# Paired value products issued as one group in alternating column halves, and a compress stage for keys and values side by side

## The chip, the cores and the metric

The kernel runs on one core of one Trainium2 chip. The metric is device time in microseconds (us), the median over runs. One execution was also recorded by the profiler; its trace gives for every engine when each instruction started and how long it took.

## The reference, cut to what matters

A two-layer decoder trunk over 256 positions with model width 1024, all in f32. Layer 0 mixes three attention groups that read one normalised input: sparse attention (8 query heads, 2 key/value groups, with a compressed branch, a selected branch and a window branch), block attention (8 heads) and attention into 256 memory rows (4 heads). Layer 1 has retention (4 heads) and memory attention again. With 256 positions the selected, window and block masks all come down to causal attention. What the change touches is this:

```python
def nsa_compress(a, pe, w1, w2):          # once for keys, once for values
    blocks = a[:, idx] + pe[...]          # 15 windows of 32 positions, stride 16
    hid = silu(einsum('bnlgd,lde->bnge', blocks, w1))
    return einsum('bnge,ef->bngf', hid, w2)

# per head, in each attention branch
p = masked_softmax(q @ k.T * scale)
o = p @ v                                 # the value product
# sparse attention: o = g0 * o_compressed + g1 * o_selected + g2 * o_window
```

## The kernel before, in words

Activations and weights of the projections are each split into two f32r parts (`split`, L102: a cast on ScalarE at L106, a subtraction on VectorE at L107), and every product is three matmuls (`mm3`, L117, lines L119 to L121). Attention probabilities and values stay f32; the trace shows every plain f32 matmul as two records, each with a weight load of its own.

Heads go in pairs. `causal_pair` (L398) does one pair of one branch: per head and per half of the queries a masked maximum on VectorE (L405), an exponential on ScalarE (L407), a scaling, then three transposes on TensorE into the only `t` bank (L178) and a copy of the bank to `pt` on ScalarE (L419). Then come four value products: for key tile 0 both heads (L421, 256 columns each), for key tile 1 both heads (L423, 128 columns each). Head 0 of the pair has 64 weight columns and writes PSUM partitions 0 to 63, head 1 writes 64 to 127, both in the bank `o`, of which there is one. `mem_attention` (L439) does the same for the memory group without a mask, with four value products of 256 columns (L469). `sparse_pair` (L577) opens its bank with the compressed branch: for each head one product from 15 rows of `vcR` and `pcT` into that head's 64 partitions (L585), and then adds two `causal_pair`s. There are four sparse pairs (two `causal_pair`s each), four block pairs (one each) and two memory pairs in each layer: 16 groups of four value products in all.

`compress` (L494) projects 280 columns, transposes, and then runs a loop over keys (i = 0) and values (i = 1): four additions on VectorE build the windows (L526), 16 accumulated matmuls with 64 weight columns and 30 moving columns (L530), then exponential, add, reciprocal and product for SiLU on 64 partitions (L533 to L537, L543), then the second weight (L538 for keys, L547 for values) and copies to `kcBD` (L540) and `vcR` (L549).

The instructions are not executed in the order of the text. The tile framework, opened with `schedule_with_timeline_sim=True` (L967), plans each engine's order at build time by simulated durations: what is ready by its simulation goes ahead, and projections fill the stretches in which attention waits. On the chip each engine then takes its instructions in that fixed order. All weights come in through SyncE's DMA queue (`load`, L86).

Of the kernel before, what the change touches and what calls it, by code (L numbers as in the profile page):

```python
# [12 lines left out]
AF = mybir.ActivationFunctionType  # L13
# [3 lines left out]
P = 128  # L17
# [34 lines left out]
def trunk(  # L52
# [33 lines left out]
    def load(t, src):  # L86
        nc.sync.dma_start(t, src)
        return t


    def rsqrt(y, v, n):
# [83 lines left out]
    def transposes(blocks, tag="t"):  # L175
        b = bank(tag)
        for i, a in enumerate(blocks):
            PE.transpose(b[:, i * P : (i + 1) * P], a, ident)  # L178
        return b[:, : P * len(blocks)]
# [218 lines left out]
    def causal_pair(ss, v, gate, o, first, last):  # L398

        p = tl("p", [P, 2, 512], 2)  # L400
        mx = tl("mx", [P, 2, 2], 3)
        sm = tl("sm", [P, 2, 2], 3)
        for hh in range(2):
            for tok, a in enumerate(SPAN):
                V.tensor_tensor_reduce(p[:, hh, a], ss[hh][tok], cpak[:, C_CAUSAL + a.start : C_CAUSAL + a.stop], -1.0,  # L405
                                       3e38, ALU.add, ALU.min, mx[:, hh, tok : tok + 1])
                S.activation(p[:, hh, a], p[:, hh, a], AF.Exp, bias=mx[:, hh, tok : tok + 1], scale=-1.0,  # L407
                             accum_out=sm[:, hh, tok : tok + 1])
        pt = tl("pt", [P, 2, 512], 2)
        for hh in range(2):  # L410
            V.reciprocal(sm[:, hh], sm[:, hh])
            if gate is not None:
                V.tensor_tensor(sm[:, hh], sm[:, hh], gate[:, :, hh], ALU.mult)
            for tok, a in enumerate(SPAN):
                if 2 * hh + tok == (0 if gate is None else 3):
                    S.activation(p[:, hh, a], p[:, hh, a], AF.Copy, scale=sm[:, hh, tok : tok + 1])
                else:
                    V.tensor_scalar(p[:, hh, a], p[:, hh, a], sm[:, hh, tok : tok + 1], None, op0=ALU.mult)
            S.copy(pt[:, hh, :384], transposes([p[:, hh, i * P : (i + 1) * P] for i in range(3)]))  # L419
        for hh in range(2):  # L420
            PE.matmul(o[hh * 64 : hh * 64 + 64, 0:T], v(hh, 0), pt[:, hh, 0:T], start=first, stop=False)  # L421
        for hh in range(2):
            PE.matmul(o[hh * 64 : hh * 64 + 64, P:T], v(hh, 1), pt[:, hh, T : T + P], start=False, stop=last)  # L423

    def gated(o, szT, y, kt):

# [12 lines left out]
    def mem_attention(eqT, kT, kl, v, szT, y):  # L439
        for pr in range(2):  # L440
# [15 lines left out]
            for hh in range(2):  # L456
                V.reciprocal(sm[:, hh], sm[:, hh])
                for tok in range(2):
                    a = slice(tok * T, (tok + 1) * T)
                    if 2 * hh + tok == 3:  # L460
                        S.activation(p[:, hh, a], p[:, hh, a], AF.Copy, scale=sm[:, hh, tok : tok + 1])
                    else:
                        V.tensor_scalar(p[:, hh, a], p[:, hh, a], sm[:, hh, tok : tok + 1], None, op0=ALU.mult)
                S.copy(pt[:, hh], transposes([p[:, hh, tok * T + kt * P : tok * T + (kt + 1) * P]
                                              for kt in range(2) for tok in range(2)]))
            for kt in range(2):
                for hh in range(2):
                    c = (2 * pr + hh) * 64
                    PE.matmul(o[hh * 64 : hh * 64 + 64, :T], v[:, kt, c : c + 64], pt[:, hh, kt * T : (kt + 1) * T],  # L469
                              start=kt == 0, stop=kt == 1)  # L470
            gated(o, szT[:, pr], y, pr)

    kS = kL = vsw = qT = nq = gates = kcBD = vcR = pcT = yn = eqS = szm = mh = ml = rstdm = rbm = memkS = memkL = memv = ym = szb = mq = mk = mkL = mvt = yb = kS1 = kL1 = v1m = None
# [20 lines left out]
    def compress():  # L494
        nonlocal gates, kcBD, vcR
        ps = project(w280, 0, (xh, xl), 280)
        w1t = [load(tl("v4", [P, 16, 64], NV), w1[i]) for i in range(2)]
        w2t = load(tl("yf", [P, T], 2)[:64, :P], w2)
        gates = tl("gates", [P, 2, 24])
        b = bank("o")  # L500
        for tok in range(2):
# [10 lines left out]

        kcBD = tl("kcbd", [P, 30])
        G.memset(kcBD, 0.0)
        srep = tl("yf", [P, T], 2)[:64].rearrange("p (g a n) -> p g a n", g=2, a=4)
        G.memset(srep, 0.0)
        vcR = tl("vcr", [P, 2, 64])
        for i in range(2):
            blk = tl("tmp2", [P, 512], 3)[:, :480].rearrange("p (a g n) -> p a g n", a=16, g=2)
            pe = vect[:, (V_PEK, V_PEV)[i] : (V_PEK, V_PEV)[i] + 32].rearrange("p (b l) -> p b l", b=2)  # L520
            for l2 in range(2):
                for g in range(2):
                    gs = slice(g * 64, (g + 1) * 64)
                    win = b[gs, i * T + l2 : i * T + T]
                    src = bass.AP(tensor=win.tensor, offset=win.offset, ap=[list(win.ap[0]), [2, 16], [16, 15]])
                    V.tensor_tensor(blk[l2 * 64 : (l2 + 1) * 64, :, g, :], src,  # L526
                                    pe[gs, l2].unsqueeze(2).to_broadcast([64, 16, 15]), ALU.add)
            hb = bank("s")
            for lp in range(16):
                PE.matmul(hb[:64, :30], w1t[i][:, lp], blk[:, lp].rearrange("p g n -> p (g n)"),  # L530
                          start=lp == 0, stop=lp == 15)
            h = tl("hid", [64, 30], 2)
            S.activation(h, hb[:64, :30], AF.Exp, scale=-1.0)  # L533
            V.tensor_scalar(h, h, 1.0, None, op0=ALU.add)
            V.reciprocal(h, h)
            if i == 0:
                V.tensor_tensor(h, hb[:64, :30], h, ALU.mult)  # L537
                PE.matmul(hb[:64, 64:94], w2t[:, 0:64], h, start=True, stop=True)  # L538
                for g in range(2):
                    S.copy(kcBD[g * 64 : (g + 1) * 64, g * 15 : (g + 1) * 15], hb[:64, 64 + g * 15 : 79 + g * 15])  # L540
            else:
                for g in range(2):
                    V.tensor_tensor(srep[:, g, :, :15],  # L543
                                    hb[:64, g * 15 : (g + 1) * 15].unsqueeze(1).to_broadcast([64, 4, 15]),
                                    h[:, g * 15 : (g + 1) * 15].unsqueeze(1).to_broadcast([64, 4, 15]), ALU.mult)
                for g in range(2):
                    PE.matmul(hb[:, 128 + g * 64 : 192 + g * 64], srep[:, g].rearrange("p a b -> p (a b)"),  # L547
                              w2t[:, 64:128], start=True, stop=True)
                S.copy(vcR.rearrange("p g f -> p (g f)"), hb[:, 128:256])  # L549

    def compressed_scores():
        nonlocal qT, gates, kcBD, pcT
# [24 lines left out]
    def sparse_pair(pr):  # L577
# [1 line left out]
        if pr == 0:  # L579
            yn = tl("y", [P, 2, 4, T], 2, F32R)  # L580
        o = bank("o")
        for g in range(2):
            n = 2 * pr + g
            cr = slice(32 * (n % 4), 32 * (n % 4) + 15)
            PE.matmul(o[g * 64 : g * 64 + 64, :T], vcR[cr, g], pcT[cr, n // 4], start=True, stop=False)  # L585
        ss = branch_scores(nq[pr // 2][:, pr % 2], kS, kL)
        for br in (1, 2):
            causal_pair(ss[br - 1],
# [382 lines left out]
```

## Time and profile before

| | |
|---|---|
| time, median of 3 runs (lowest to highest) | 450.48 us (450.01 to 451.08) |
| the profiled execution: its own time | 450.25 us |
| its span, first to last instruction | 448.5 us |
| around the span | 1.75 us |
| TensorE busy, records | 435.9 us (97%), 2586 |
| weight loads busy | 367.8 us (82%) |
| VectorE busy | 331.7 us (74%) |
| ScalarE busy | 257.3 us (57%) |
| GpSimd busy | 9.4 us (2%) |
| mean granted TensorE clock | 0.997 |

Busy time of TensorE counts the whole of each record, and records overlap, since the next matmul starts while the one before is still draining. So 97% doesn't say that the array streams all that time: what a matmul costs is read from the distance between the starts of two that follow each other.

### The profile page before, as it was taken

How to read it: one execution, taken by the hardware profiler on the slowest of the kernel's cores; microseconds unless marked ns; L12 is line 12 of the kernel's file. 1: busy time of each engine (PE TensorE's matmuls, PEld its weight loads, DVE VectorE, ACT ScalarE, POOL GpSimd, SP SyncE). 2: the span in 40 equal slices, each digit the busy share in tenths (PEclk: the TensorE clock that was granted, in tenths of full speed). 3: DMA queues.
4: the chain of work that ended last, by engine and by line, in shares of the span. 5: the costliest groups of instructions: out<-in, count | busy, mean ns of one | idle time of the engine just before them, and what ended most of it. 6: DMA issues, size and time to landing. Idle time of an engine off the chain costs nothing.

```text
span 448.5 us, 7101 instructions
## 1 busy us (share of the span) xinstructions
PE 435.9 (97%) x2586; PEld 367.8 (82%) x2586; DVE 331.7 (74%) x762; ACT 257.3 (57%) x472; POOL 9.4 (2%) x22
## 2 busy tenths in 40 slices
PE   8999999999999799999999999999999999999994
PEld 6988899888777467667999888888998888888883
DVE  4898989997888766756898776577877478764725
ACT  5756557947656966854646625464543356453714
POOL 0000100001101000000010000000000000000000
PEclk9999999999999999999999999999999999999998
DMA  8965765853343134222546334455545545555402
GB/s 281 391 227 185 214 235 176 274 187 134 102 142 132 56 117 165 95 94 95 176 145 214 142 117 166 164 178 160 190 145 186 187 142 203 159 209 198 142 0 94
DMA packets 22146, 74.20 MB, mean 165 GB/s; under 512 B 2720, under 2 KB 3424, under 8 KB 22112
## 3 DMA queue, kind: packets, MB, share of 16 engines
q1 hardware_dynamic: 21536, 72.92, 47.1%
q10 hardware_dynamic: 576, 0.84, 0.6%
q8 instruction: 20, 0.33, 0.3%
q14 instruction: 14, 0.11, 0.1%
HBM read 72.70 MB, written 1.05 MB: 164 GB/s over the span
## 4 chain that ended last, share of the span: by engine, by line
PE 91%; DVE 3%; ACT 3%; DMA 1%; issue 1%; ACTq 0%
PE pj L119 23%; PE pj L120 23%; PE pj L121 22%; PE t L178 3%; PE o L421 2%; PE s L372 1%; PE s L120 1%; PE s L119 1%; PE o L469 1%; PE s L121 1%; PE tr L120 1%; PE tr L119 1%; PE s L373 1%; PE tr L121 1%; DMA vec<-in_vec 1%
## 5 line engine op out<-in xcount | busy, mean ns | idle before, releaser
L107 DVE TENSOR_TENSOR wlo<-raw,whi 128x1024 fp32r<-128x1024 f32 (+2 forms) x124 | 145.1, 1174 | 58.2 <-ACT whi L106 57.2
L106 ACT CAST whi<-raw 128x1024 fp32r<-128x1024 f32 (+2 forms) x124 | 124.6, 1007 | 94.0 <-PE pj L121 28.0
L120 PE MATMUL pj<-wlo,big 128*128 128x512 f32 (+2 forms) x264 | 99.0, 375 | 0.1
L121 PE MATMUL pj<-whi,big 128*128 128x512 f32 (+2 forms) x264 | 98.3, 373 | 0.0
L119 PE MATMUL pj<-whi,big 128*128 128x512 f32 (+2 forms) x264 | 92.7, 376 | 0.0
L119 PE MATMUL pj<-big,whi 128*128 128x256 f32 x288 | 80.6, 285 | 0.7 <-ACT big L198 0.6
L120 PE MATMUL pj<-big,whi 128*128 128x256 f32 x288 | 81.1, 285 | 0.0
L121 PE MATMUL pj<-big,wlo 128*128 128x256 f32 x288 | 80.0, 285 | 0.5 <-DVE wlo L107 0.4
L120 PEld LDWEIGHTS pj<-wlo,big 128*128 128x128 f32 x264 | 49.7, 188 | 9.1 <-issue 0.8
L119 PEld LDWEIGHTS pj<-big,whi 128*128 128x128 f32 x288 | 54.7, 191 | 2.5 <-ACT big L198 1.0
L121 PEld LDWEIGHTS pj<-whi,big 128*128 128x128 f32 x264 | 49.7, 188 | 8.4
L119 PEld LDWEIGHTS pj<-whi,big 128*128 128x128 f32 x264 | 49.2, 188 | 8.4 <-issue 0.4
L120 PEld LDWEIGHTS pj<-big,whi 128*128 128x128 f32 x288 | 55.0, 191 | 0.8 <-issue 0.4
L121 PEld LDWEIGHTS pj<-big,wlo 128*128 128x128 f32 x288 | 54.3, 191 | 1.0 <-DVE wlo L107 0.9
L407 ACT ACTIVATE p<-p,mx 128x256 f32<-128x256 f32 (+1 forms) x48 | 21.4, 448 | 1.5 <-DVE mx L405 1.3
L178 PE MATMUL t<-cst,p 128*128 128x128 f32 x104 | 18.0, 281 | 1.0 <-ACT pt L419 0.6
L405 DVE CUSTOM_DVE_ANT_0 p<-s,cst 128x256 f32<-128x256 f32 (+1 forms) x48 | 14.6, 353 | 4.9 <-PE t L178 4.4
L419 ACT COPY pt<-t 128x384 f32<-128x384 f32 x24 | 11.5, 479 | 10.7 <-PE t L178 10.6
L178 PEld LDWEIGHTS t<-cst,p 128*128 128x128 f32 x104 | 11.8, 140 | 6.0 <-issue 3.3
L372 PE MATMUL s<-v,v 128*128 128x256 f32 (+2 forms) x48 | 14.7, 326 | 0.2 <-DVE mx L405 0.2
L120 PE MATMUL pj<-wlo,y 128*128 128x512 f32 x36 | 14.2, 396 | 0.0
L373 PE MATMUL s<-v,v 128*128 128x256 f32 (+2 forms) x48 | 13.4, 298 | 0.0
(292 smaller groups left out, 649.5 us busy)
## 6 DMA issues: line engine op xcount, KB each, us to landing
raw<-in_w SPq DMA_DIRECT2D x91, 512.0 KB, 3.8
raw<-in_wout SPq DMA_DIRECT2D x28, 512.0 KB, 3.6
v<-in_xtok SPq DMA_DIRECT2D x4, 512.0 KB, 6.2
raw<-in_w SPq DMA_DIRECT2D x4, 280.0 KB, 3.4
v<-in_w SPq DMA_DIRECT2D x2, 512.0 KB, 7.0
raw<-in_memT SPq DMA_DIRECT2D x2, 512.0 KB, 3.5
raw<-in_memtok SPq DMA_DIRECT2D x2, 512.0 KB, 4.6
v<-in_grow SPq DMA_DIRECT2D x2, 512.0 KB, 5.5
```

Of the source, the lines that this page charges most:

```text
L106: S.copy(hi, raw)
L107: V.tensor_tensor(lo, raw, hi.bitcast(F32), ALU.subtract)
L119: PE.matmul(ps, lh, rh, start=start, stop=False, skip_group_check=shared)
L120: PE.matmul(ps, lh, rl, start=False, stop=False, skip_group_check=shared)
L121: PE.matmul(ps, ll, rh, start=False, stop=stop, skip_group_check=shared)
L178: PE.transpose(b[:, i * P : (i + 1) * P], a, ident)
L372: PE.matmul(s, q, k, start=True, stop=False)
L373: PE.matmul(s, q, kl, start=False, stop=True)
L405: V.tensor_tensor_reduce(p[:, hh, a], ss[hh][tok], cpak[:, C_CAUSAL + a.start : C_CAUSAL + a.stop], -1.0, 3e38, ALU.add, ALU.min, mx[:, hh ...
L407: S.activation(p[:, hh, a], p[:, hh, a], AF.Exp, bias=mx[:, hh, tok : tok + 1], scale=-1.0, accum_out=sm[:, hh, tok : tok + 1])
L419: S.copy(pt[:, hh, :384], transposes([p[:, hh, i * P : (i + 1) * P] for i in range(3)]))
L421: PE.matmul(o[hh * 64 : hh * 64 + 64, 0:T], v(hh, 0), pt[:, hh, 0:T], start=first, stop=False)
```

## The change

The four value products of a pair become one list that is handed to a new helper, `side_by_side`. It issues them in the same order as the lines before (key tile 0 of head 0, of head 1, key tile 1 of head 0, of head 1), but ties the first to the second head's `pt` copy by an explicit dependency, and each later one behind the one before it on TensorE. The compressed branch of a sparse pair becomes one matmul with 128 weight columns: `vcR` is now 128 x 2 x 128 with zeros outside the blocks, so that the product of head g uses its own 15 rows alone. In `compress` the two loops of 16 matmuls are interleaved, keys into partitions 0 to 63 and values into 64 to 127 of one bank; SiLU runs once on 128 partitions; `w2` is loaded twice, once for each half of the partitions; `vcR` is cleared on GpSimd and filled by four copies.

```diff
@@ -86,6 +86,21 @@
     def load(t, src):
         nc.sync.dma_start(t, src)
         return t
+
+    def after(ins, *others):
+
+        for other in others:
+            tc.add_manual_dep(ins.ins, other.ins.name,
+                              mybir.DependencyInfo(mybir.DependencyClass.Sync, mybir.DependencyReason.DATA), reason="pair")
+
+    def side_by_side(todo, *others):
+
+        for i, (out, lhs, rhs, start, stop) in enumerate(todo):
+            ins = PE.matmul(out, lhs, rhs, start=start, stop=stop)
+            if i == 0:
+                after(ins, *others)
+            else:
+                tc.keep_in_program_order(ins)
 
 
     def rsqrt(y, v, n):
@@ -416,11 +431,9 @@
                     S.activation(p[:, hh, a], p[:, hh, a], AF.Copy, scale=sm[:, hh, tok : tok + 1])
                 else:
                     V.tensor_scalar(p[:, hh, a], p[:, hh, a], sm[:, hh, tok : tok + 1], None, op0=ALU.mult)
-            S.copy(pt[:, hh, :384], transposes([p[:, hh, i * P : (i + 1) * P] for i in range(3)]))
-        for hh in range(2):
-            PE.matmul(o[hh * 64 : hh * 64 + 64, 0:T], v(hh, 0), pt[:, hh, 0:T], start=first, stop=False)
-        for hh in range(2):
-            PE.matmul(o[hh * 64 : hh * 64 + 64, P:T], v(hh, 1), pt[:, hh, T : T + P], start=False, stop=last)
+            got = S.copy(pt[:, hh, :384], transposes([p[:, hh, i * P : (i + 1) * P] for i in range(3)]))
+        side_by_side([(o[hh * 64 : hh * 64 + 64, kt * P : T], v(hh, kt), pt[:, hh, kt * T : kt * P + T],
+                       first and kt == 0, last and kt == 1) for kt in range(2) for hh in range(2)], got)
 
     def gated(o, szT, y, kt):
 
@@ -461,13 +474,10 @@
                         S.activation(p[:, hh, a], p[:, hh, a], AF.Copy, scale=sm[:, hh, tok : tok + 1])
                     else:
                         V.tensor_scalar(p[:, hh, a], p[:, hh, a], sm[:, hh, tok : tok + 1], None, op0=ALU.mult)
-                S.copy(pt[:, hh], transposes([p[:, hh, tok * T + kt * P : tok * T + (kt + 1) * P]
-                                              for kt in range(2) for tok in range(2)]))
-            for kt in range(2):
-                for hh in range(2):
-                    c = (2 * pr + hh) * 64
-                    PE.matmul(o[hh * 64 : hh * 64 + 64, :T], v[:, kt, c : c + 64], pt[:, hh, kt * T : (kt + 1) * T],
-                              start=kt == 0, stop=kt == 1)
+                got = S.copy(pt[:, hh], transposes([p[:, hh, tok * T + kt * P : tok * T + (kt + 1) * P]
+                                                    for kt in range(2) for tok in range(2)]))
+            side_by_side([(o[hh * 64 : hh * 64 + 64, :T], v[:, kt, (2 * pr + hh) * 64 : (2 * pr + hh + 1) * 64],
+                           pt[:, hh, kt * T : (kt + 1) * T], kt == 0, kt == 1) for kt in range(2) for hh in range(2)], got)
             gated(o, szT[:, pr], y, pr)
 
     kS = kL = vsw = qT = nq = gates = kcBD = vcR = pcT = yn = eqS = szm = mh = ml = rstdm = rbm = memkS = memkL = memv = ym = szb = mq = mk = mkL = mvt = yb = kS1 = kL1 = v1m = None
@@ -495,7 +505,9 @@
         nonlocal gates, kcBD, vcR
         ps = project(w280, 0, (xh, xl), 280)
         w1t = [load(tl("v4", [P, 16, 64], NV), w1[i]) for i in range(2)]
-        w2t = load(tl("yf", [P, T], 2)[:64, :P], w2)
+        w2t = tl("yf", [P, T], 2)[:, :P]
+        for i in range(2):
+            load(w2t[64 * i : 64 * i + 64], w2)
         gates = tl("gates", [P, 2, 24])
         b = bank("o")
         for tok in range(2):
@@ -512,9 +524,11 @@
 
         kcBD = tl("kcbd", [P, 30])
         G.memset(kcBD, 0.0)
-        srep = tl("yf", [P, T], 2)[:64].rearrange("p (g a n) -> p g a n", g=2, a=4)
+        srep = tl("yf", [P, T], 2)[64:].rearrange("p (g a n) -> p g a n", g=2, a=4)
         G.memset(srep, 0.0)
-        vcR = tl("vcr", [P, 2, 64])
+        vcR = tl("vcr", [P, 2, 2, 64])
+        G.memset(vcR, 0.0)
+        blks = []
         for i in range(2):
             blk = tl("tmp2", [P, 512], 3)[:, :480].rearrange("p (a g n) -> p a g n", a=16, g=2)
             pe = vect[:, (V_PEK, V_PEV)[i] : (V_PEK, V_PEV)[i] + 32].rearrange("p (b l) -> p b l", b=2)
@@ -523,30 +537,29 @@
                     gs = slice(g * 64, (g + 1) * 64)
                     win = b[gs, i * T + l2 : i * T + T]
                     src = bass.AP(tensor=win.tensor, offset=win.offset, ap=[list(win.ap[0]), [2, 16], [16, 15]])
-                    V.tensor_tensor(blk[l2 * 64 : (l2 + 1) * 64, :, g, :], src,
-                                    pe[gs, l2].unsqueeze(2).to_broadcast([64, 16, 15]), ALU.add)
-            hb = bank("s")
-            for lp in range(16):
-                PE.matmul(hb[:64, :30], w1t[i][:, lp], blk[:, lp].rearrange("p g n -> p (g n)"),
-                          start=lp == 0, stop=lp == 15)
-            h = tl("hid", [64, 30], 2)
-            S.activation(h, hb[:64, :30], AF.Exp, scale=-1.0)
-            V.tensor_scalar(h, h, 1.0, None, op0=ALU.add)
-            V.reciprocal(h, h)
-            if i == 0:
-                V.tensor_tensor(h, hb[:64, :30], h, ALU.mult)
-                PE.matmul(hb[:64, 64:94], w2t[:, 0:64], h, start=True, stop=True)
-                for g in range(2):
-                    S.copy(kcBD[g * 64 : (g + 1) * 64, g * 15 : (g + 1) * 15], hb[:64, 64 + g * 15 : 79 + g * 15])
-            else:
-                for g in range(2):
-                    V.tensor_tensor(srep[:, g, :, :15],
-                                    hb[:64, g * 15 : (g + 1) * 15].unsqueeze(1).to_broadcast([64, 4, 15]),
-                                    h[:, g * 15 : (g + 1) * 15].unsqueeze(1).to_broadcast([64, 4, 15]), ALU.mult)
-                for g in range(2):
-                    PE.matmul(hb[:, 128 + g * 64 : 192 + g * 64], srep[:, g].rearrange("p a b -> p (a b)"),
-                              w2t[:, 64:128], start=True, stop=True)
-                S.copy(vcR.rearrange("p g f -> p (g f)"), hb[:, 128:256])
+                    got = V.tensor_tensor(blk[l2 * 64 : (l2 + 1) * 64, :, g, :], src,
+                                          pe[gs, l2].unsqueeze(2).to_broadcast([64, 16, 15]), ALU.add)
+            blks.append(blk)
+
+        hb = bank("s")
+        side_by_side([(hb[64 * i : 64 * i + 64, :30], w1t[i][:, lp], blks[i][:, lp].rearrange("p g n -> p (g n)"),
+                       lp == 0, lp == 15) for lp in range(16) for i in range(2)], got)
+        h = tl("hid", [P, 30])
+        S.activation(h, hb[:, :30], AF.Exp, scale=-1.0)
+        V.tensor_scalar(h, h, 1.0, None, op0=ALU.add)
+        V.reciprocal(h, h)
+        V.tensor_tensor(h, hb[:, :30], h, ALU.mult)
+        for g in range(2):
+            V.tensor_copy(srep[:, g, :, :15], h[64:, g * 15 : (g + 1) * 15].unsqueeze(1).to_broadcast([64, 4, 15]))
+        PE.matmul(hb[:64, 64:94], w2t[:64, 0:64], h[:64], start=True, stop=True)
+        for g in range(2):
+            PE.matmul(hb[:, 128 + g * 64 : 192 + g * 64], srep[:, g].rearrange("p a b -> p (a b)"),
+                      w2t[64:, 64:128], start=True, stop=True)
+        for g in range(2):
+            S.copy(kcBD[g * 64 : (g + 1) * 64, g * 15 : (g + 1) * 15], hb[:64, 64 + g * 15 : 79 + g * 15])
+        for a in range(4):
+            rows = slice(32 * a, 32 * a + 15)
+            S.copy(vcR[rows, a // 2, a % 2], hb[rows, 128 + 64 * (a % 2) : 192 + 64 * (a % 2)])
 
     def compressed_scores():
         nonlocal qT, gates, kcBD, pcT
@@ -579,10 +592,7 @@
         if pr == 0:
             yn = tl("y", [P, 2, 4, T], 2, F32R)
         o = bank("o")
-        for g in range(2):
-            n = 2 * pr + g
-            cr = slice(32 * (n % 4), 32 * (n % 4) + 15)
-            PE.matmul(o[g * 64 : g * 64 + 64, :T], vcR[cr, g], pcT[cr, n // 4], start=True, stop=False)
+        PE.matmul(o[:, :T], vcR[:, pr % 2].rearrange("p g f -> p (g f)"), pcT[:, pr // 2], start=True, stop=False)
         ss = branch_scores(nq[pr // 2][:, pr % 2], kS, kL)
         for br in (1, 2):
             causal_pair(ss[br - 1],
```

## Rows read from the trace of the kernel before

**Rows 1.** The page: busy tenths in 40 slices of the span, 11.2 us each.

```profile
PE   8999999999999799999999999999999999999994
DVE  4898989997888766756898776577877478764725
```

**Rows 2.** TensorE's waits: for whom, us in total, times, longest.

```profile
PE o L469 <- ACT pt L464: 1.4, 1, 1.4
PE o L421 <- ACT pt L419: 0.8, 2, 0.6
```

**Rows 3.** Windows by stage: busy PE, PEld, DVE, ACT, POOL; clock, DMA.

```profile
58.00:95.00 37.00, 37.00 (x293) 34.33 (x292) 35.34 (x97) 26.09 (x56) 0.84 (x2) 1.00 0.65 221
95.00:150.00 55.00, 54.21 (x321) 41.65 (x322) 46.13 (x125) 35.89 (x88) 4.57 (x10) 1.00 0.40 133
150.00:165.00 15.00, 12.94 (x73) 7.90 (x72) 9.87 (x41) 12.81 (x42) 0.00 (x0) 1.00 0.06 17
165.00:205.00 40.00, 39.15 (x203) 27.96 (x204) 23.20 (x78) 23.73 (x62) 0.00 (x0) 1.00 0.40 139
205.00:264.00 59.00, 58.91 (x463) 55.23 (x462) 47.44 (x82) 34.30 (x60) 1.42 (x2) 1.00 0.42 147
```

**Rows 4.** Chain that ended last: first and last short burst, and one behind L585.

```profile
99.69 0.58 PE o L421 x2
...
143.43 0.58 PE o L585 x4
144.01 0.57 PE o L421 x2
...
259.29 0.57 PE o L469 x2
```

**Rows 5.** Timeline of TensorE, a short burst: start, us, line.

```profile
98.97 0.28 PE L119 MATMUL pj<-whi,big 128*128 128x256 f32 x1
99.09 0.60 PE L178 MATMUL tr<-cst,rot_a 128*128 128x128 f32 x4
99.62 0.65 PE L421 MATMUL o<-pt,s 128*64 128x256 f32 x2
100.19 0.38 PE L120 MATMUL pj<-wlo,big 128*128 128x256 f32 x1
100.41 0.28 PE L121 MATMUL pj<-whi,big 128*128 128x256 f32 x1
```

**Rows 6.** Timeline of TensorE, the long burst of the same pair.

```profile
104.90 0.43 PE L421 MATMUL o<-pt,s 128*64 128x256 f32 x1
104.91 0.43 PE L423 MATMUL o<-pt,s 128*64 128x128 f32 x2
105.17 0.38 PE L421 MATMUL o<-pt,s 128*64 128x256 f32 x1
105.39 0.38 PE L423 MATMUL o<-pt,s 128*64 128x128 f32 x2
105.70 0.55 PE L178 MATMUL t<-cst,p 128*128 128x128 f32 x3
```

**Rows 7.** Timeline of TensorE, the compressed branch.

```profile
95.51 0.65 PE L585 MATMUL o<-s,vcr 15*64 15x256 f32 x4
96.09 0.55 PE L178 MATMUL t<-cst,p 128*128 128x128 f32 x3
```

**Rows 8.** Timeline of TensorE, first matmuls of the compress stage.

```profile
62.36 3.92 PE L530 MATMUL s<-tmp,v 128*64 128x30 f32 x64
66.20 0.39 PE L120 MATMUL pj<-big,whi 128*128 128x256 f32 x1
```

**Rows 9.** Timelines of VectorE and ScalarE in the compress stage.

```profile
66.42 0.33 DVE L535 RECIPROCAL hid<-hid 64x30 f32<-64x30 f32 x1
...
70.94 0.34 ACT L540 COPY kcbd<-s 64x15 f32<-64x15 f32 x2
...
78.55 0.24 ACT L549 COPY vcr<-s 128x128 f32<-128x128 f32 x1
```

## The prediction

> **What bounds the kernel now.** I read the page first. The busy tenths [rows 1] show TensorE at 9 in nearly every slice, and the mean granted clock is 0.997, so nothing is to be won or lost by the clock. The waits of TensorE [rows 2] come next: the ones in the middle of the span are small, and they are waits for a `pt` copy of ScalarE. Then the windows by stage [rows 3], which say what stands ready to bind behind TensorE: VectorE is busy 95.5% of 58 to 95 us (35.34 of 37) while TensorE still never rests there, and 84% from 95 to 150; ScalarE is busy 85% from 150 to 165, the one stretch in which TensorE loses 2 us; from 165 to 264 the next engine has at most 80% (47.44 of 59). Last the chain that ended last [rows 4]: it runs through TensorE nearly everywhere, so that time taken from TensorE there is time off the span, until VectorE or ScalarE takes its place.
>
> The chain also names the target. Short bursts of two records with 64 weight columns (L421 or L469, "x2") stand on it 13 times between 99.69 and 259.29, at 0.57 to 0.58 us each; I show the first, one of the two that directly follow L585, and the last [rows 4]. They are the value product of a pair's first head for key tile 0, which the planner put out as soon as that head's `pt` was copied, long before the second head's. Three more lie off the chain (near 149.0, 153.3 and 180.2 us): 16 in all, one for each group of four products.
>
> **What one short burst costs.** The first is at 99.62 [rows 5]. Plain f32r matmuls start 0.12 apart (98.97, 99.09). Four transposes from 99.09 at 0.11 each (half the 0.22 that a pass of twice the columns takes, 105.17 to 105.39 in [rows 6]) would let the next start at 99.53; it starts at 99.62: 0.09 to 0.10 lost on entering the half-array form. From its first start to the next full-width matmul 0.57 (99.62 to 100.19). The one after that comes 0.22 later and not 0.12 (100.19 to 100.41): 0.10 lost after leaving. So 0.57 + 0.10 + 0.10 = 0.77 us for two passes that hold 2 x 0.22 us of streaming.
>
> **What the second burst costs, and why the first goes for nothing.** Five us later the same pair's other six records follow [rows 6]: L421 of one head at 104.90, L423 of the other at 104.91 and again 0.16 later, L421's second pass at 105.17, then L423 of the first head, and the next full-width matmul at 105.70: 0.80 us. The halves run beside each other: while one streams 256 columns, the other takes two passes of 128. One half is full (0.05 + 0.22 + 0.22 + 0.11 + 0.11, and 0.10 to leave, is 0.80), and the other stands idle where head 0's key tile 0 could have run. With all eight records in one group each half has 256, 256, 128, 128 columns: the same 0.80 us. So the change removes 0.77 us per group and adds nothing in streaming.
>
> By the Trainium skill ("TensorEngine Tiling (Array Packing)", Key Properties) changing the tiling mode drains TensorE. The 0.10 us on either side of the burst fit that; the sum above uses the rows alone.
>
> **The sum on TensorE.**
> A. 11 bursts on the chain that stand alone: 11 x 0.77 = 8.5 us.
> B. 2 on the chain that follow L585 without a change of form: 2 x 0.58 = 1.2 us.
> C. 3 off the chain, where ScalarE's copy ended the wait: 0 to 0.58 each; I take 0 and keep 1.7 for the range.
> D. The compressed branch, four times. Two heads of two passes each take 0.58 from 95.51 to 96.09 [rows 7], with 0.10 before and 0.10 after: 0.77, as above (where L421 followed, that loss was not counted in B). As one full-width product it is two passes of 0.22, 0.44, with no change of form: 4 x 0.33 = 1.3 us.
> E. The compress stage: 64 records from 62.36 to the next matmul at 66.20 are 3.84 us, 0.06 each [rows 8]. Their 30 columns can't take that, by the 0.11 for 128; the weight load does. No row shows 64 records on alternating halves. Ends: 0 (loads take turns) and 1.9 us (each half keeps its own 0.06). The nearest row is the start of the six-record burst, where the halves start 0.01 apart [rows 6], which speaks for the upper end; as two orders of halves never ran that long, I take 1.2.
> Sum: 8.5 + 1.2 + 0 + 1.3 + 1.2 = 12.2 us.
>
> **What the edit adds elsewhere.** VectorE loses one add, one reciprocal of 0.33 and one product [rows 9], about 0.7 us in a stretch where it is nearly full. ScalarE gets four copies for one of 0.24, at about 0.17 each by the nearest small copy (two in 0.34) [rows 9], less one exponential: +0.3 us, between -0.2 and +0.8, where it is 71% busy (26.09 of 37 [rows 3]). GpSimd clears `vcR`; it has 0.84 us of work in 37 [rows 3]. SyncE's queue issues one more DMA of `w2` ahead of the weight loads behind it; TensorE has no wait for weights there, as `raw` has six buffers. I cost these at nothing; without that cover they are under 1 us. The values' `vcR` and the keys' `kcBD` now hang on both window sets, but the 64 matmuls already stood in one unbroken block behind the last set [rows 8], so neither starts later.
>
> The added wait: the group's first product waits for the second head's copy, and everything behind it on TensorE waits too. Three of the six-record products per group already wait for that copy, and their longest waits are 1.4 and 0.6 us [rows 2]. Head 0's product no longer fills time before it; projections must, and there the planner has them except around 143 to 165.
>
> **What is late next.** From 58 to 150 us the sum takes 4 x 0.77 + 0.58 + 3 x 0.33 + 1.2 = 5.9 us from 92. VectorE has 35.34 + 46.13 - 0.7 = 80.8 us there, so it would have to be busy 94%, just under the 95.5% it reaches with TensorE at full [rows 3]. It can, with no slack left for an order fixed at build time; I count 70% of the 5.9 and lose 1.7. From 150 to 165 ScalarE ends the waits; of the 1.7 us there I count half and lose 0.8. The 4.6 us from 165 to 264 I count in full. Net 12.2 - 1.7 - 0.8 = 9.7: the profiled execution's 450.25 becomes **440.5 us**. The median of the runs is 0.23 higher, which I leave out.
>
> **The rivals.**
> 1. *The next engine takes half.* VectorE from 58 to 150 and ScalarE's copies to 165 give back everything there, and the planner's new order costs as much as E: only the 4.6 us behind 165 stay, 445.6. For: the 95.5% and the 85% [rows 3]. Against: TensorE keeps up at 95.5%.
> 2. *The passes start in strict order.* The Trainium skill ("TensorE: Matmul & The Clock Gate", Part 3, "What overlaps and what doesn't") says that matmuls start and end in program order. As a mechanism here: head 1's first pass could not start before head 0's second, and the group's eight passes come in a staircase: 0, 0.27, 0.28, 0.49, 0.50, 0.61, 0.62, 0.73 and out at 0.94, so 0.14 more for 12 groups, about 0.22 more for four groups of 256 columns, and half of E: 1.7 + 0.9 + 0.6, 443.7 us. Against: L423's second record starts ahead of L421's second [rows 6], and the four records of L585 end 0.65 after the first start where a staircase needs 0.9 [rows 7].
> 3. *TensorE stands at the group* (slower). With head 0's product gone from before the copy, the planner has nothing to put there, and TensorE stands for the copy chain at each group, as once today for 1.36 us, the 1.4 of [rows 2]. It decides from 0.6 us more per group (9.7 / 16); at 0.9 us it is 14.4 - 9.7 = 4.7 us slower, 455. For: the explicit wait, and one `t` bank for both heads' transposes. Against: at 13 of 16 groups the chain runs through TensorE, with projections right behind the burst.
> 4. *The halves take turns after all* (the change doesn't do what it says): each group of 12 is 1.4 us for 0.80 and each of four 1.9 for 1.0, 10.8 us that eat A and B; with D about 450. [rows 6] and [rows 7] speak against it.
>
> **How the numbers follow.** Chances: forecast 0.65, with its own range 435.5 (all of 12.2, C's 1.7 and the rest of E) to 443; rival 1 0.18; rival 2 0.05; rival 3 0.08; rival 4 0.02; 0.02 that gains and losses cancel within what can be told from no change, 0.2% or 0.9 us. The range is 435.5 to 447.0: it takes in rivals 1 and 2 and leaves out 3, 4 and the null case. Faster 0.88, same 0.04, slower 0.08.
>
> **What would show it.** Right: no more bursts of two; 12 groups of eight records with 64 weight columns that reach the next matmul in 0.80 us, four in 1.0; the compressed branch as two records 0.22 apart with no 0.10 before them; the compress block under 3 us; VectorE near 94% from 58 to 150. Wrong: idle time of TensorE that ends with `pt` copies and exceeds 5 us in all (rival 3); groups of 0.94 (rival 2) or 1.4 (rival 4); idle time that ends with VectorE's splits (rival 1). The forecast fails above all if TensorE's time falls by 12 us and its idle time rises by the same.

## The result

The changed kernel takes 445.17 us (median of 4 runs, 444.31 to 446.00) against 450.25 us for the kernel before, measured beside it: a ratio of 0.9883, with a 95% interval of 0.9862 to 0.9903. It is 5.1 us faster; 9.7 were forecast. The time lies 0.4 us from that of rival 1 (445.6), in which only the 4.6 us behind 165 us stay. The profiled execution took 444.31 us (span 442.5).

**The profile after.** The busy tenths of the page (PE, DVE; [rows 1] before):

```profile
PE   7999999999997799899999999999999999999994
DVE  4898989898898675847888775787778487764725
```

Two slices of TensorE at 7 (133 to 155 us) stand where one stood (146 to 157). The windows by stage, in the columns of [rows 3]:

```profile
58.00:95.00 37.00, 37.00 (x308) 34.28 (x307) 34.89 (x86) 25.76 (x54) 0.83 (x2) 1.00 0.68 229
95.00:150.00 55.00, 50.96 (x317) 41.22 (x316) 48.81 (x141) 39.88 (x102) 6.58 (x10) 1.00 0.40 126
150.00:165.00 15.00, 12.95 (x68) 9.24 (x69) 10.74 (x41) 11.76 (x34) 0.00 (x0) 0.89 0.20 63
165.00:205.00 40.00, 37.24 (x213) 28.21 (x212) 24.51 (x75) 24.56 (x63) 0.00 (x0) 1.00 0.40 135
205.00:264.00 59.00, 59.00 (x472) 56.67 (x471) 49.57 (x85) 34.19 (x62) 1.42 (x2) 1.00 0.49 156
```

TensorE now rests 4.0 us of 95 to 150, where it rested 0.8, and the granted clock of 150 to 165 is 0.89 on average, where it was 1.00. VectorE is busy 91% from 58 to 150 (34.89 + 48.81 of 92): short of the 94% that I had worked out, and of the 95.5% it had reached. TensorE's waits on attention that are new or longer ([rows 2] before):

```profile
PE o L99 <- ACT pt L477: 1.9, 1, 1.9
PE o L99 <- ACT pt L434: 1.7, 3, 0.6
PE t L193 <- ACT pt L434: 1.5, 3, 0.6
PE t L193 <- DVE p L433: 1.4, 1, 1.4
PE pj L134 <- ACT y L442: 1.0, 1, 1.0
PE s L387 <- DVE mx L420: 0.7, 1, 0.7
```

In these six rows TensorE waits on attention, on ScalarE and VectorE by turns: 8.2 us. Its other four waits add up to 3.0 us, where the same four were 2.6 before. Waits that end with a `pt` copy are now 5.4 us in all (1.9 + 1.7 + 1.5, and 0.3 that was there before), where they were 3.1. The matmuls themselves do what the working said (timelines of TensorE; `side_by_side` issues at L99, the compressed branch is L595):

```profile
62.89 2.06 PE L99 MATMUL s<-tmp,v 128*64 128x30 f32 x64
64.88 0.39 PE L136 MATMUL pj<-big,wlo 128*128 128x256 f32 x1
...
97.02 0.60 PE L595 MATMUL o<-s,vcr 128*128 128x256 f32 x2
97.26 0.47 PE L135 MATMUL pj<-wlo,big 128*128 128x256 f32 x1
97.57 0.28 PE L136 MATMUL pj<-whi,big 128*128 128x256 f32 x1
...
107.70 0.87 PE L99 MATMUL o<-pt,s 128*64 128x256 f32 x8
108.50 0.44 PE L193 MATMUL t<-cst,p 128*128 128x128 f32 x2
```

No burst of two is left; all 16 groups have eight records. A group of eight reaches the next matmul in 0.80 us (107.70 to 108.50), as the six-record burst did [rows 6]; the 64 records of the compress stage reach it in 1.99 us (62.89 to 64.88), against 3.84 [rows 8]. The compressed branch's two records and the matmul behind them take 0.55 us (97.02 to 97.57), which is the 0.44 worked out and 0.11 for that matmul.

**Where the time went.** One event splits the span: the first matmul of the first output projection, which needs the memory group's output `ym`. The last projection matmul ahead of it started at 143.04 us before and starts at 134.25 now: 8.8 us sooner. The first matmul on `ym` itself (before, then after):

```profile
157.36 0.50 PE L119 MATMUL pj<-whi,ym 128*128 128x512 f32 x1 [0.43 <-ACT ym L429]
```

```profile
152.59 1.97 PE L99 MATMUL o<-pt,s 128*64 128x256 f32 x8 [1.94 <-ACT pt L477]
154.50 1.12 PE L193 MATMUL t<-cst,p 128*128 128x128 f32 x4
155.55 0.80 PE L193 MATMUL tr<-cst,rot_a 128*128 128x128 f32 x4
156.10 0.47 PE L134 MATMUL pj<-whi,ym 128*128 128x512 f32 x1
```

It is 1.3 us sooner (157.36 to 156.10). Behind it the span has 286.4 us left where it had 291.1: 4.7 us less. Ahead of `ym` TensorE ran out of projections and stood on attention. The last lines also show a price I hadn't put down: right behind the 1.94 us wait the group of eight takes 1.91 us to the next matmul and not 1.0. The granted clock is mostly at its lower level, 1.2 GHz, there (busy times, clock, DMA as above):

```profile
154.00:156.00 2.00, 2.00 (x11) 1.17 (x8) 1.68 (x5) 0.96 (x3) 0.00 (x0) 0.53 0.00 0
```

### The profile page after: what moved, and what is told of

It is laid out like the page before. It is cut to its first block, busy times and chain, and to the rows that moved or that the text cites. A ratio compares the mean times of both kernels' runs of the same rounds, so it can differ in the third digit from the quotient of the medians.

```text
span 442.5 us, 7082 instructions
## 1 busy us (share of the span) xinstructions
PE 424.5 (96%) x2578; PEld 364.6 (82%) x2578; DVE 331.9 (75%) x760; ACT 257.8 (58%) x474; POOL 11.7 (3%) x23
## 4 chain that ended last, share of the span: by engine, by line
PE 89%; DVE 4%; ACT 4%; DMA 1%; issue 1%; ACTq 0%
PE pj L134 23%; PE pj L135 23%; PE pj L136 23%; PE t L193 4%; PE o L99 3%; PE s L135 1%; PE s L134 1%; PE s L136 1%; PE tr L134 1%; PE tr L135 1%; DMA vec<-in_vec 1%; PE s L387 1%; PE tr L136 1%; PE s L388 1%; PE s L796 1%
## 5 line engine op out<-in xcount | busy, mean ns | idle before, releaser
L99 PE MATMUL o<-pt,s 128*64 128x256 f32 (+1 forms) x96 | 12.2, 378 | 3.8 <-ACT pt L477 1.9
L387 PE MATMUL s<-v,v 128*128 128x256 f32 (+2 forms) x48 | 14.6, 324 | 0.9 <-DVE mx L420 0.7
L340 POOL CAST v<-v 64x256 fp32r<-64x256 f32 (+1 forms) x14 | 9.8, 699 | 193.2 <-DVE v L339 193.2
```

What stands on the lines that cost most here:

```text
L99: ins = PE.matmul(out, lhs, rhs, start=start, stop=stop)
L340: G.tensor_copy(lo[other, :, i], lo[own, :, i].bitcast(F32))
L387: PE.matmul(s, q, k, start=True, stop=False)
```

## The experiments

Each row is one kernel: its median; from its profiled execution the start of the first compressed score (TensorE's product with `kcBD`), the start of the first matmul on `ym`, and the span left behind that. The profiled executions of e9 and e10 took 1.4 us less than their medians and that of e11 took 2.0 us more, the longest of its six; the others lie within 0.9 us.

| kernel | median us | first `kcBD` product | first on `ym` | span behind |
|---|---|---|---|---|
| before | 450.25 | 73.18 | 157.36 | 291.1 |
| changed | 445.17 | 78.83 | 156.10 | 286.4 |
| e1, products alone | 442.94 | 72.84 | 155.08 | 286.5 |
| e2, compress and branch alone | 451.56 | 78.22 | 159.63 | 289.9 |
| e3, changed, block projections later | 454.23 | 82.21 | 167.25 | 285.9 |
| e4, before, block projections later | 460.98 | 80.98 | 169.17 | 290.1 |
| e6, changed, head by head | 444.91 | 78.19 | 156.58 | 286.5 |
| e8, products and branch | 442.82 | 73.02 | 153.40 | 287.7 |
| e9, changed, two chains | 446.19 | 80.00 | 157.10 | 285.9 |
| e10, changed, chain ranked first | 445.19 | 78.20 | 155.43 | 286.5 |
| e11, e8 with the keys made to wait | 446.60 | 79.59 | 159.63 | 287.2 |
| e12, e8 with a filled wait | 441.42 | 72.83 | 154.35 | 285.3 |
| e13, e8 with value copies on VectorE | 441.14 | 73.12 | 153.58 | 285.9 |
| e14, e13 without the copy wait | 448.38 | 72.87 | 156.78 | 289.8 |

**The two halves of the change.** e1 takes the value products of the diff and leaves `compress` and L585 as before; e2 is the other half.

> The kernel before with the grouped value products alone; the compress stage and the compressed branch stay as they were. In the changed kernel the last projection matmul of layer 0 starts 8.8 us earlier than before (134.25 for 143.04), but the first matmul of the output projection only 1.3 us earlier (156.10 for 157.36). Theory A (no filler): until the memory group's output is ready the chain of attention through VectorE and ScalarE sets the pace, and what TensorE saves ahead of that is waited away; behind it every short burst that is gone counts, six of 0.77 us. A expects about 445.7 us, nearly the whole gain of the change. Theory B (VectorE's rate): VectorE is full from 58 to 150 and the 0.7 us that the compress part takes from it is worth as much as that; B expects about 446.5.

> The changed kernel with the value products as they were (first head early, no group); the compress stage side by side and the compressed branch as one matmul stay. Its TensorE saves 1.9 us at 62 to 66 and about 0.33 four times, nearly all ahead of the memory group's output. Theory A: that is waited away before the output projection can start; 449.5 to 450.2, no change. Theory B: VectorE's 0.7 us and part of TensorE's 3 us count: 448 to 449.5.

e1: 442.94 us, 0.9833 of the kernel before (0.9815 to 0.9852). e2: 451.56 us, 1.0036 (1.0014 to 1.0057). Neither theory had this: the products alone are worth 7.1 us, and the compress part, which takes over 3 us from TensorE, costs time. The times of e2's twelve runs go with their mean granted clock: the five at 0.995 to 0.996 took 450.1 to 451.6 us, the two lowest, at 0.986, took 454.1 and 454.6, and five lie between. So at a nearly full clock e2 is near the kernel before, and what it loses beyond that goes with the clock.

**Is it projections to fill with?** In e3 and e4 two calls move:

```diff
     compressed_scores()
-    block_gates()
-    block_keys()
     memory_rows()
     for pr in range(3):
         sparse_pair(pr)
     memory_scale()
     memory_keys()
     memory_group()
+    block_gates()
+    block_keys()
     block_queries()
```

> The changed kernel with one thing moved: the calls of block_gates and block_keys (the gate and key projections of the block attention, with their work on VectorE) stand behind memory_group in the text, so that the planner ranks the sparse and memory attention ahead of them. Theory A: attention starts earlier, projections are left to fill its waits, the memory output is ready earlier and TensorE hardly idles between 95 and 200; the 5 us of added idle time and the 1.7 us of half clock go: 437 to 440 us. Theory B: VectorE has the same work and is as full, only in another order: 444 to 446.

> The kernel before with the same two calls moved. Theory A: it idles 3.4 us around the memory group and gets most of that back, 446 to 448 us, and against it the change is then worth 8 to 10 us (the run with the same order and the change) and not 5. Theory B: 450, and the change is worth 5 us in either order.

454.23 us (1.0079, 1.0053 to 1.0105) and 460.98 us (1.0226, 1.0202 to 1.0251): both theories missed both times. By the trace the move takes the filler from where it was needed, in the compress stage. TensorE's two longest waits in e3:

```profile
PE s L99 <- DMA v<-in_w: 2.7, 2, 1.8
PE pj L136 <- DVE wlo L122: 2.0, 1, 2.0
```

Both lie between 52 and 68 us, and attention doesn't start sooner, since its first products hang on `kcBD` (82.21 us in the table). In that order the change is worth 6.8 us (460.98 to 454.23), between A's 8 to 10 and B's 5. The late `kcBD` pointed at the next suspect, the compress chain.

**Why the compress part costs.** Ahead of the `kcBD` products stand the keys' SiLU, their second weight and two copies. On ScalarE, the kernel before and then the changed kernel:

```profile
64.44 0.19 ACT L533 ACTIVATE hid<-s 64x30 f32<-64x30 f32 x1 [0.18 <-PE s L530]
...
70.94 0.34 ACT L540 COPY kcbd<-s 64x15 f32<-64x15 f32 x2
```

```profile
66.69 0.20 ACT L548 ACTIVATE hid<-s 128x30 f32<-128x30 f32 x1
...
76.86 0.33 ACT L559 COPY kcbd<-s 64x15 f32<-64x15 f32 x2
```

Before, the keys' exponential ran while the values' matmuls still streamed. Now it comes 2.2 us later, and the copies 5.9 us later: in the changed kernel's timelines other work's casts and splits stand between one link and the next on VectorE and ScalarE. Four runs go after it. e10 wraps the chain and `compressed_scores()` in the planner's high priority. e8 is e1 with the padded `vcR` and the single branch product, but the old two loops of `compress`. e9 keeps the interleaved matmuls and runs the chain twice, keys first, second products in a bank of their own:

```diff
-        S.activation(h, hb[:, :30], AF.Exp, scale=-1.0)
...
+        kb = bank("s")
+        for i in range(2):
+            r = slice(64 * i, 64 * i + 64)
+            S.activation(h[r], hb[r, :30], AF.Exp, scale=-1.0)
...
+            if i == 0:
+                V.tensor_tensor(h[r], hb[r, :30], h[r], ALU.mult)
+                PE.matmul(kb[:64, 64:94], w2t[:64, 0:64], h[:64], start=True, stop=True)
```

> The changed kernel with the planner told to rank the compress stage's chain (from SiLU on) and the compressed scores ahead of other ready work; no instruction is added or taken. In the changed kernel the keys' copies to kcBD come at 76.86 us, against 70.94 before, and with them the compressed scores 5.6 us later, though the 64 matmuls end 1.3 us earlier. Theory C (late chain): keys and values share one chain, each link of it queues behind other work on ScalarE and VectorE, and attention starts late; that is why the products alone take 442.94 us and the whole change 445.17. C expects kcBD before 74 us and 442.0 to 443.5. Theory D (the padded branch): the zero-padded vcR with its four copies and the 128-wide product cost the 2.2 us; D expects 445, whatever the rank.

> The kernel with the grouped value products alone, plus the padded vcR (cleared on GpSimd, filled by four copies) and the compressed branch as one full-width product; the compress stage keeps its two loops, one after the other, and its two chains. Theory C: the branch gives back its 0.33 us four times at most and costs nothing, 441.6 to 443.0. Theory D: 444.5 to 445.5, as the whole change.

> The changed kernel with the matmuls side by side as they are, but behind them two chains again: SiLU, second weight and kcBD for the keys on partitions 0 to 63, then the same for the values on 64 to 127, the second weights' products in a bank of their own. Theory C: kcBD comes earlier than 76.86 us by what the values' links took, and the time falls towards 442 to 443.5. Theory D: 445. If kcBD comes no earlier, it is the rank of the chain in the planner's order and not its length, and the time stays at 445.

e8: 442.82 us (0.9839, 0.9826 to 0.9851), as e1: theory D, that the padded branch costs, falls; the branch gains nothing either. e10: 445.19 (0.9887, 0.9867 to 0.9907): the copies come at 76.95 and not 76.86, so the rank changed nearly nothing in the planned order and nothing in the time, and it doesn't test C. e9: 446.19 (0.9925, 0.9911 to 0.9939), slower than either theory had it: `kcBD` is copied at 75.33, 1.5 us sooner than in the changed kernel, but its products start only at 80.00. To put the suspect to the test, e11 adds the wait to e8. To name the last of the values' 16 matmuls, it also splits the loop, so that the keys' chain stands behind those matmuls in the text (in part):

```diff
-                PE.matmul(hb[:64, :30], w1t[i][:, lp], blk[:, lp].rearrange("p g n -> p (g n)"),
-                          start=lp == 0, stop=lp == 15)
+                got = PE.matmul(hb[:64, :30], w1t[i][:, lp], blk[:, lp].rearrange("p g n -> p (g n)"),
+                                start=lp == 0, stop=lp == 15)
+            hbs.append(hb)
+        for i in range(2):
+            hb = hbs[i]
...
-            S.activation(h, hb[:64, :30], AF.Exp, scale=-1.0)
+            ins = S.activation(h, hb[:64, :30], AF.Exp, scale=-1.0)
+            if i == 0:
+                after(ins, got)
```

> The kernel with grouped products, padded branch and two separate compress chains (442.82 us), with one wait added: the keys' exponential waits for the last of the values' 16 matmuls, as it does in the changed kernel. No instruction is added or taken. Theory C (late chain: the keys' part of compress waits for the values' part, and attention starts late by it): kcBD later than 70.8 us by 2 us or more, the memory output later, 444 to 445.5 us. If the wait makes no difference, 442.8, the 2.2 us lie elsewhere in the joint stage (its 128-partition SiLU, the second load of w2, the copies).

446.60 us (0.9924, 0.9906 to 0.9943), 3.8 us more than e8 and 1.1 beyond what C had. ScalarE in e8 and in e11:

```profile
64.28 0.19 ACT L545 ACTIVATE hid<-s 64x30 f32<-64x30 f32 x1 [0.19 <-PE s L542]
67.14 0.19 ACT L545 ACTIVATE hid<-s 64x30 f32<-64x30 f32 x1
70.79 0.34 ACT L552 COPY kcbd<-s 64x15 f32<-64x15 f32 x2
```

```profile
66.96 0.27 ACT L549 ACTIVATE hid<-s 64x30 f32<-64x30 f32 x2
76.39 0.34 ACT L558 COPY kcbd<-s 64x15 f32<-64x15 f32 x2
```

With the wait, and no instruction added or taken, `kcBD` goes from 70.79 to 76.39, about the place it has in the changed kernel. The memory group's first value products go from 151.31 to 154.32, released by a `pt` copy of ScalarE both times, and the first matmul on `ym` from 153.40 to 159.63 in this execution, the longest of six. Theory C is shown as a mechanism: a keys' chain that stands behind the values is late, and lateness there reaches `ym`. A run with the loop split and without the wait isn't there, so the two aren't told apart. Part of the 3.8 us goes with the clock: the e11 run at 0.997 took 445.39, the four e8 runs at 0.993 to 0.994 took 442.54 to 442.97.

The traces also show where the filler goes. In e1, e8, e12 and e13, with the keys' chain as before, the last projection matmul ahead of `ym` starts at 139.3 to 139.8 us; in the changed kernel, e2, e6, e9, e10 and e11, with the chain late, at 133.6 to 135.9.

**What paces the memory group, and what the clock costs.** Both edits start from e8. Its TensorE and ScalarE at the memory group:

```profile
151.31 1.08 PE L100 MATMUL o<-pt,s 128*64 128x256 f32 x8 [1.93 <-ACT pt L478]
153.40 0.80 PE L135 MATMUL pj<-whi,ym 128*128 128x512 f32 x1 [0.23 <-ACT ym L443]
...
149.53 1.26 ACT L661 ACTIVATE v<-pj,rstd 128x512 f32<-128x512 f32 x2
150.68 0.57 ACT L478 COPY pt<-t 128x512 f32<-128x512 f32 x1
```

e12 fills the 1.93 us wait ahead of the group's first value products (`hold` is 8 in layer 0 and 0 in layer 1); e13 moves the two L661 copies from ScalarE to VectorE. The first two lines are e12's, the last two e13's:

```diff
+            for _ in range(hold if pr == 0 else 0):
+                tc.keep_in_program_order(PE.matmul(o[:, :P], ident, ident, start=True, stop=True))
...
-            S.activation(mvt[:, tok], ps[tok], AF.Copy, scale=rstd0[:, tok : tok + 1])
+            V.tensor_scalar(mvt[:, tok], ps[tok], rstd0[:, tok : tok + 1], None, op0=ALU.mult)
```

> The same kernel (442.82 us) with eight products of the identity with itself (128 columns, about 1.8 us) put on TensorE where it stands 1.93 us for the second head's copy in the memory group's first pair, into the bank that the group then overwrites. The granted clock falls to half at 152.7 us, 3.4 us long, right behind that idle stretch. If the clock is what it costs, it stays at full, the matmuls to 156 take their full-speed time, and 1 to 1.7 us go: 441.1 to 441.9. If something else paces that stretch (the copies of ScalarE), the clock stays up and the time stays: 442.6 to 443.

> The same kernel (442.82 us) with the two scaled copies of the block attention's values (0.63 us each) on VectorE and not on ScalarE. On ScalarE they stand ahead of the second head's pt copy, for which TensorE waits 1.93 us at the memory group (149.4 to 151.3 us), and VectorE rests 1.4 us there. If ScalarE's order paces the stretch up to the memory output, the wait falls to about 0.7 us, the clock stays at full, and the time goes to 440 to 441.5. If it is VectorE, the output projection starts as late: 442.5 to 443.5.

e12: 441.42 us (0.9808, 0.9795 to 0.9821). TensorE in it:

```profile
149.06 1.95 PE L481 MATMUL o<-cst 128*128 128x128 f32 x16
151.16 1.08 PE L100 MATMUL o<-pt,s 128*64 128x256 f32 x8
152.17 0.65 PE L194 MATMUL t<-cst,p 128*128 128x128 f32 x4
153.50 0.66 PE L194 MATMUL t<-cst,p 128*128 128x128 f32 x4 [0.68 <-ACT pt L478]
```

The group takes 1.01 us again (151.16 to 152.17) and no record is stretched; the granted clock of 150 to 165 us is 1.00, where e8 had 0.89. Idle work bought 1.4 us: that is what the lower clock cost in e8. e13: 441.14 us (0.9801, 0.9788 to 0.9814); its TensorE, then ScalarE's copy:

```profile
150.30 1.08 PE L100 MATMUL o<-pt,s 128*64 128x256 f32 x8 [0.79 <-ACT pt L478]
151.31 0.66 PE L194 MATMUL t<-cst,p 128*128 128x128 f32 x4
153.58 0.50 PE L135 MATMUL pj<-whi,ym 128*128 128x512 f32 x1 [0.17 <-ACT ym L443]
...
149.66 0.58 ACT L478 COPY pt<-t 128x512 f32<-128x512 f32 x1
```

The wait is 0.79 us and not 1.93, and the clock stays up without help. ScalarE's order, not VectorE's rate, made the long wait: the `pt` copy stood behind the two L661 copies. But neither edit brings `ym` forward: its first matmul starts at 153.58 in e13 and 154.35 in e12, against 153.40 in e8. What they win lies behind it (285.9 and 285.3 us left, against 287.7), and goes with the clock; what sets the start of `ym` they don't show. e13 beats both kernels, by 9 us and by 4 us.

**What merges the bursts.** e14 drops `got` from the two calls of `side_by_side` in e13, so that a group's first product waits for its own head alone.

> The kernel with grouped products, padded branch, separate compress chains and the value copies on VectorE (441.14 us), with one thing taken out: the first product of a group no longer waits for the second head's pt copy, only for its own head's. The chaining of the others behind it stays. If that wait is what merges the two bursts, the planner puts the first head's product out early again: short bursts of two records at 0.77 us each are back on the chain, up to 13 of them, and the time goes up by 5 to 9 us, to 446 to 450. If the chaining alone merged them, the time stays within 1 us.

448.38 us (0.9955, 0.9941 to 0.9968), 7.2 us more than e13. Its chain has all 13 short bursts back, of which the first and the last:

```profile
99.75 0.58 PE o L100 x2
...
257.35 0.57 PE o L100 x2
```

The added wait is the useful edit: it keeps the planner from putting out the first head early.

**Does the alternation matter?** e6 turns the two loops of the list round.

> The changed kernel with one thing turned round: in each group the four value products are issued head by head (key tiles 0 and 1 of head 0, then of head 1) and not in alternating halves. If each column half works through its own products whatever the order of issue, a group still reaches the next matmul in 0.80 us (1.0 in the memory group), 445 us in all. If matmuls start in order of issue, head 1 starts when head 0's last pass has: 0.05 + 0.22 + 0.22 + 0.11 + 0.05 for head 0, then 0.66 for head 1 and 0.10 to leave, about 1.3 us for 12 groups and 1.7 for four: 0.5 x 12 + 0.7 x 4 = 9 us more on TensorE, of which some hides in its waits: 449 to 454.

444.91 us (0.9885, 0.9873 to 0.9898), as the changed kernel:

```profile
107.07 0.88 PE L99 MATMUL o<-pt,s 128*64 128x256 f32 x8
107.88 0.55 PE L193 MATMUL t<-cst,p 128*128 128x128 f32 x3
```

0.81 us to the next matmul, with both products of head 0 issued ahead of head 1's. The order in a group makes no difference.

## Why the prediction was right, and where not

The direction and the range held; the forecast itself, 440.5, was 4.7 us too low. That the time lies on rival 1's is in part luck: rival 1 names neither a late keys' chain nor the clock, which the runs show to be costs of this change.

- **The price of a short burst** (0.77 us, A and B): as worked out on TensorE, since a group of eight takes what the six-record burst took. In time, all 16 gone are worth 7.2 us in e13 against e14 and 7.1 in e1, where the 13 on the chain were put at 9.7 ahead of any discount.
- **Groups at no extra streaming**: right, 0.80 us for eight records as for six. Rivals 2 and 4 are out, by the group and by e6.
- **E**: the upper end was right, 1.85 us and not the 1.2 I took. **D**: the branch's two records are as worked out, but e8 against e1 shows no gain in time.
- **Behind `ym`**: right. 4.6 us counted in full from 165 to 264; the span behind the first matmul on `ym` is 4.7 us shorter.
- **Ahead of `ym`**: here the sum failed. 7.6 us of TensorE's work were counted down to 5.1; 1.3 came. The step "what is late next" asked how busy VectorE would be, a rate. What the trace shows is a chain: the softmax steps of one pair after another through VectorE, ScalarE and the single `t` bank up to `ym`, with too few projections left to fill it. No engine is full in that stretch (VectorE 89%, ScalarE 73% of 95 to 150). Most of the shortfall goes with the joined compress stage: e8, with the same products and branch, has its first matmul on `ym` 4.0 us sooner than the kernel before, near the 4.1 that the discounted sum leaves there without E (70% of 4.65, and half of 1.7); in e12 and e13 it is 3.0 and 3.8. And e12, with the clock held as well, is 8.5 us faster than the kernel before, measured beside it (449.93); 9.7 less E's discounted 0.8 is 8.9. Whether this agreement is more than luck isn't shown. Rival 1 had the time and the stretch right, and named VectorE's rate and ScalarE's copies; e13 shows that the copies made the long wait, and no run shows that VectorE's rate cost anything.
- **The sign of rival 3**: it came, 5.4 us of waits that end with `pt` copies, where over 5 was to tell against the forecast. But 3.1 of them were there before, and the 2.3 us on top are far from rival 3's 14.4; the sign was set too low to tell the two apart.
- **"So neither starts later"**: wrong, and the costliest sentence. It looked at the start of the 64 records. The keys' chain behind them had run inside the values' matmuls (64.44 us, after the block's start at 62.36 [rows 8]); joined, it begins behind all of them and its copies come 5.9 us later. The whole change is 2.2 us slower than its products alone.
- **"Nothing is to be won or lost by the clock"**: wrong, and a term put at nothing. It held for the profiled execution before, but already that kernel's runs differ: beside e1, three at 0.992 took 450.9 to 451.4 us, those at 0.997 to 0.999 took 449.8 to 450.3. In the changed kernel TensorE stands longer and the clock falls behind it: 0.89 over 150 to 165 us is 1.65 us of full-speed time in the profiled execution, and from e8, with the same 0.89, e12 got 1.4 back.

The books close roughly: the waits that the trace lists for TensorE rose by some 5 us (6.0 to 11.2), the clock took 1.65, and 5.9 us are left of the profiled time (450.25 to 444.31). Together that is 12 to 13 us, the sum on TensorE with E at what it measured (12.9).

Two things stay open. Whether the interleaved compress matmuls can pay at all: in every kernel that had them the keys' chain was late, and no order of the planner's was found in which it wasn't. And how the 2.2 us divide between the late chain itself and the clock that falls with it: at a mean clock of 0.996 to 0.997 single runs of e10, whose copies to `kcBD` come within 0.1 us of the changed kernel's, took 443.41, of e1 442.48 and 442.83, and e12 took about 441.4, so that 0.6 to 2.0 us is left to the chain by which of them it is set against.

## What to carry to other kernels

Time taken from the engine that is busy everywhere counts where it has other work to go on with; ahead of a point that hangs on a long chain through other engines (here `ym`) ask what that chain does, link by link, and not how busy its engines are. Joining two independent chains makes the one that is needed first wait for the other, and here each link that slipped came later still behind other work. When an edit leaves the tensor engine standing, look at the granted clock behind the gap.

## What the runs showed of the hardware

- The two column halves work through their own matmuls whatever the order of issue: 0.81 us for a group issued head by head, 0.80 in alternation. The Trainium skill ("TensorE: Matmul & The Clock Gate", Part 3, "What overlaps and what doesn't") has matmuls start in program order. The trace doesn't agree for two column halves: in strict order e6's group would have taken about 1.3 us, the estimate ahead of that run, and it took 0.81.
- 64 records of 30 columns in alternating halves keep one half's spacing each: 1.99 us for what took 3.84 in one half.
- The granted clock went to its lower level behind a stretch of thin work with a 1.94 us wait at its end; the same wait in e9's profiled execution, at 0.996, brought no such fall, while e9's other five runs had mean clocks of 0.986 to 0.992. With the wait filled, all five runs of e12 stood at 0.996 to 0.998.
